# Low parts of layer A's weights by DMAs that add, in a two-layer decoder trunk on one core

## The chip, the cores and the metric

The kernel runs on one core of one Trainium2 chip. The metric is the device time of one execution in microseconds; the median of three runs before the change is 933.11 us (932.33 to 933.43).

## What is computed

x has 512 rows of 1024. Layer A is a retention layer with 4 heads, layer B a latent attention with 16 heads; each ends in a layer norm of a scaled residual sum. The change lies in layer A:

```python
def _retention_layer(x, w_in, w_out):
    b, s, _ = x.shape
    hproj = x @ w_in
    qk = H_A * DK_A
    q = hproj[..., :qk].reshape(b, s, H_A, DK_A)
    k = hproj[..., qk:2 * qk].reshape(b, s, H_A, DK_A)
    v = hproj[..., 2 * qk:2 * qk + WIDTH_A].reshape(b, s, H_A, DV_A)
    gate = hproj[..., 2 * qk + WIDTH_A:]
    q = _rope(q, ROPE_BASE_A)
    k = _rope(k, ROPE_BASE_A) * (DK_A ** -0.5)
    o = _chunkwise_retention(q, k, v)
    ...
    return (o * jax.nn.silu(gate)) @ w_out
```

All of it is float32; H_A = 4, DK_A = 256, DV_A = 512.

## The kernel before, in words

**Three products for one.** Every float32 matrix is split in two parts of a shorter float type: the high part is a cast, the low part what the cast left out. A product is then three matmuls of TensorE that add up in PSUM: high by high, high by low, low by high (`mm3`, lines 97 to 99; the first projection has its own loop, line 387).

**Weights.** All weights pass through the class `Weights` as tiles of 128 x 1024. For each, SP loads a staging tile `wst` (line 65, or 48 in `load`), ScalarE casts it to `whi` (line 66) and VectorE or GpSimd writes `wlo` = `wst` - `whi` (line 68). GpSimd gets every third tile, from the ninth on, unless its name is in `on_vector`. The pairs `whi`, `wlo` rotate through four buffers, so a tile's pair can be written once TensorE has done with the tile four earlier; staging has eight buffers in layer A. `get` hands a tile to its user and issues two tiles ahead.

**Layer A, head by head.** For the values and gates of a head (`values_and_gates`), x and the two weight blocks are cut in quarters, and seven products take the place of eight: p1, p6, p2, p5, p7, p4, p3 in this order, each of two weight tiles (24 matmuls). Some of them use sums of weights, built in staging tiles by `w_vg` (line 118): for p6, v0 = g0 - v0 and then t2 = g1 - v0; for p4, v1 = v1 - t2 (`last_sum`); for p7, g0 = g1 - g0. In head 0, t2 lies in the spare buffers `wsum`, which later hold s4, the fourth form of x. In head 0 these sums are VectorE's; in heads 1 to 3 GpSimd does the last two kinds. Forms of x (s1 to s4) are summed and split on VectorE and ScalarE. After p2 come the scores of the head (24 matmuls of 512 to 128 columns; `sf`, `sTh`, `sTl`), then p5, p7, p4, p3, the inner products (30 matmuls), and with `proj_qk` the query and key of the next head (`qk1` and on, four tiles of 24 matmuls), the transposes and the output projection (`o0` and on, four tiles). In head 0 the rows of x are loaded again for the residual (line 569), after the second of the next weight loads, and scaled by ScalarE (line 571).

**What sets the order.** The program is written head by head, and a scheduler that works from its own costs then fixes each engine's order of instructions, SP's and GpSimd's queues included. An engine goes through its list in order: what stands behind a waiting instruction waits too.

Of the kernel before, what the change touches and what calls it, by code (L numbers as in the profile page):

```python
# [8 lines left out]
F32 = mybir.dt.float32  # L9
BF16 = mybir.dt.bfloat16  # L10
F32R = mybir.dt.float32r
AF = mybir.ActivationFunctionType
ALU = mybir.AluOpType
# [6 lines left out]
H_A, DK_A, DV_A = 4, 256, 512  # L20
# [16 lines left out]
class Weights:  # L37
# [3 lines left out]
    def __init__(self, nc, stage, parts, ahead):  # L41
        self.nc, self.stage, self.parts, self.ahead = nc, stage, parts, ahead
        self.todo, self.ready, self.n, self.place = [], [], 0, {}
        self.on_vector = {f"p{i}.0" for i in range(1, 8)} | {f"p{i}.3" for i in (7, 4, 3)} | {"o3", "lat"}

    def load(self, ap):
        st = self.stage.tile([P, WC], F32, tag="wst", name="wst")
# [3 lines left out]
    def issue(self, between=None):  # L51


        nc = self.nc
        name, aps, n = self.todo.pop(0)
        st = aps() if callable(aps) else self.stage.tile([P, WC], F32, tag="wst", name="wst")
        pool, th, tl = self.place[name].pop(0) if self.place.get(name) else (self.parts, "whi", "wlo")
        hi = pool.tile([P, WC], F32R, tag=th, name="whi")
        lo = pool.tile([P, WC], F32R, tag=tl, name="wlo")
        for j, ap in enumerate(aps if isinstance(aps, list) else [aps]):  # L60
            sl = slice(j * n, (j + 1) * n)
            if j and between:
                between()
            if not callable(ap):
                self.last = nc.sync.dma_start(st[:, sl], ap)
            nc.scalar.copy(hi[:, sl], st[:, sl])  # L66
            eng = nc.gpsimd if self.n % 3 == 2 and self.n > EAGER and name not in self.on_vector else nc.vector
            eng.tensor_tensor(out=lo[:, sl], in0=st[:, sl], in1=hi.bitcast(F32)[:, sl], op=ALU.subtract)  # L68
        self.n += 1
        self.ready.append((name, hi, lo))  # L70
# [10 lines left out]
def trunk_kernel(ctx, tc, a):  # L81
    nc = tc.nc
    out = a["out"]
# [26 lines left out]
    def w_vg(h):  # L110

        v, g, s = a["w_v"], a["w_g"], {}

        def sub(out, x, y, eng):
            eng.tensor_tensor(out=out, in0=x, in1=y, op=ALU.subtract)  # L118
            return out

        def p1(t):
            s["v0", t] = W.load(v[4 * h + t])
            return s["v0", t]

        def p6(t):
            s["g0", t] = W.load(g[4 * h + t])
            s["g1", t] = W.load(g[4 * h + 2 + t])
            sub(s["v0", t], s["g0", t], s["v0", t], nc.vector)


            s["t2", t] = spare.pop(0) if spare else s["g1", t]
            return sub(s["t2", t], s["g1", t], s["v0", t], nc.vector)

        def p2(t):
            s["v1", t] = W.load(v[4 * h + 2 + t])
            return s["v1", t]

        def last_sum(t):
            return sub(s["v1", t], s["v1", t], s["t2", t], nc.gpsimd if h else nc.vector)

        def p5(t):
            if h:
                last_sum(t)
            return s["v0", t]

        def p7(t):
            if s["t2", t] is s["g1", t]:
                s["g1", t] = W.load(g[4 * h + 2 + t])
            return sub(s["g0", t], s["g1", t], s["g0", t], nc.gpsimd if h else nc.vector)

        def p4(t):
            return s["v1", t] if h else last_sum(t)

        def p3(t):
            return s["g1", t]

        def entry(f, t):
            return (f"{f.__name__}.{h}", lambda: f(t), 1024)

        return [entry(f, t) for f in (p1, p6, p2, p5, p7, p4, p3) for t in range(2)]  # L160

    spare = []

    order = [("qk0", [a["w_qk0"][2 * c], a["w_qk0"][2 * c + 1]], 512) for c in range(KX // 2)]
    for h in range(H_A):
        order += w_vg(h)
        if h + 1 < H_A:
            order += [(f"qk{h + 1}", a["w_qk"][4 * h + t], 1024) for t in range(4)]
        order += w_a("w_ao", "o", h)
# [23 lines left out]
    for p in range(NP):  # L193
        i, b = 2 * p, 2 * p + 1
# [123 lines left out]
    if True:  # L318
# [51 lines left out]
        qk, vv, sT, gs, oT, dec, ors = {}, {}, {}, {}, {}, {}, {}  # L370
# [210 lines left out]
        g1 = keep.tile([P, D], F32, tag="lng", name="g1")  # L581
# [107 lines left out]
    with tc.tile_pool(name="pb1", bufs=1) as p1:  # L689
# [33 lines left out]
        for c in range(4):  # L723
            wh, wl = W.get("ql0")
            for n in ORD:
                for j in range(2):
                    k = 2 * c + j
                    sl = slice(j * 512, (j + 1) * 512)
# [3 lines left out]
        for n in range(NT):  # L732
            y = p1.tile([P, QL], F32, tag="qn", name="qn", bufs=4)
# [5 lines left out]
        for c, ks in enumerate(((0, 1, 2), (3, 4, 5), (6, 7))):  # L739
            wh, wl = W.get("ql1")  # L740
            for n in range(NT):
                for j, k in enumerate(ks):
                    sl = slice(j * 320, (j + 1) * 320)
# [162 lines left out]
    for p in range(NP):  # L906
        i, b = 2 * p, 2 * p + 1
# [62 lines left out]
    st = p2.tile([P, 4, 6], F32, tag="ln_st4", name="ln_st4")  # L970
# [11 lines left out]
    for sl in (slice(0, 512), slice(512, 1024)):  # L982
        y = r[:, last, sl]
        nc.vector.scalar_tensor_tensor(out=y, in0=y, scalar=mv[:, 0:1], in1=g2[:, sl], op0=ALU.subtract, op1=ALU.mult)
    for sl, queue in ((slice(0, 512), nc.sync), (quarters[2], nc.scalar), (quarters[3], nc.sync)):
        y = r[:, last, sl]
# [101 lines left out]
```

## Time and profile before

| | |
|---|---|
| median of three runs | 933.11 us |
| the profiled execution | 931.95 us, its span 930.1 us |
| TensorE busy | 913.4 us (98%), 4553 matmuls |
| VectorE busy | 647.0 us (70%) |
| ScalarE busy | 356.9 us (38%) |
| GpSimd busy | 176.5 us (19%) |
| DMA | 97.45 MB, mean 105 GB/s |

PE is TensorE, PEld its weight loads, DVE VectorE, ACT ScalarE, POOL GpSimd, SP the engine that issues the loads. Times in rows are microseconds from the start of the span. Matmuls overlap (one starts before the last has ended), so a row's duration of 0.39 us is not the step from one to the next. Head 0's products end at 84 us, its projections at some 130; head 3's products begin near 318, and layer A ends near 400.

### The profile page before, as it was taken

Reading aid. Unit: us, or ns where it says so; the run is one execution under the profiler, and the core shown is the slowest. Engines: PE = TensorE matmul, PEld = TensorE weight load, DVE = VectorE, ACT = ScalarE, POOL = GpSimd, SP = SyncE. Lnnn points to the kernel's source line nnn. Section 1 sums busy time; section 2 is a strip of 40 time slices with the busy share of each in tenths; the row PEclk is TensorE's granted clock in tenths of the full one; section 3 lists DMA queues with packets and bytes.
Section 4 is the critical chain, followed back from the end, with each engine's and each line's share of the span. In section 5 each row is a group of like instructions: output and inputs, shape, how many; then the busy total and the mean of one; then the engine's idle time right before and its main releaser. Section 6 shows DMA issues by size and latency. Waiting matters only on the chain.

```text
span 930.1 us, 11970 instructions
## 1 busy us (share of the span) xinstructions
PE 913.4 (98%) x4553; PEld 774.6 (83%) x4553; DVE 647.0 (70%) x1117; ACT 356.9 (38%) x600; POOL 176.5 (19%) x108
## 2 busy tenths in 40 slices
PE   9989999999999999999999999999999999999996
PEld 6767888888888887888988888888888888888885
DVE  7998767866796689952477476564865648657577
ACT  6463334333433344222525443333433334334431
POOL 0001136212631250121312011010011011111204
PEclk9999999999999999999999999999999999999998
DMA  9164204420442050134143324242242422423212
GB/s 335 61 220 145 89 30 141 159 91 16 152 161 91 12 203 24 68 88 136 52 125 117 105 74 123 75 125 69 74 136 68 119 69 74 135 70 108 92 69 91
DMA packets 32362, 97.45 MB, mean 105 GB/s; under 512 B 4272, under 2 KB 4912, under 8 KB 32304
## 3 DMA queue, kind: packets, MB, share of 16 engines
q1 hardware_dynamic: 28800, 87.11, 27.8%
q10 hardware_dynamic: 3504, 9.57, 4.0%
q8 instruction: 36, 0.59, 0.3%
q14 instruction: 22, 0.18, 0.1%
HBM read 86.18 MB, written 2.10 MB: 95 GB/s over the span
## 4 chain that ended last, share of the span: by engine, by line
PE 81%; DVE 8%; issue 4%; POOL 3%; DMA 3%; ACT 1%; SPq 0%; DVEq 0%; POOLq 0%; ACTq 0%
PE ps L98 25%; PE ps L99 25%; PE ps L97 25%; DVE wlo L68 2%; PE ps L848 2%; POOL wst L118 1%; DMA wst<-in_w_v 1%; PE ps L825 1%; PE ps L826 1%; DMA r<-in_xT 1%; DMA r<-in_x 1%; PE ps L540 1%; POOL wlo L68 1%; PE ps L302 1%; DVE vl L103 0%
## 5 line engine op out<-in xcount | busy, mean ns | idle before, releaser
L66 ACT CAST whi<-wst 128x1024 fp32r<-128x1024 f32 (+3 forms) x181 | 173.2, 964 | 264.0 <-PE ps L98 89.1
L68 DVE TENSOR_TENSOR wlo<-wst,whi 128x1024 fp32r<-128x1024 f32 (+2 forms) x132 | 163.2, 1241 | 96.9 <-ACT whi L66 96.4
L68 POOL TENSOR_TENSOR wlo<-wst,whi 128x1024 fp32r<-128x1024 f32 (+3 forms) x49 | 110.6, 2257 | 615.8 <-ACT whi L66 584.6
L833 ACT ACTIVATE p<-ps,sm 128x512 f32<-128x512 f32 (+1 forms) x64 | 33.3, 525 | 66.6 <-DVE sm L830 66.5
L97 PE MATMUL ps<-qlt_h,whi 128*128 128x512 f32 x144 | 56.9, 395 | 0.0
L98 PE MATMUL ps<-qlt_l,whi 128*128 128x512 f32 x144 | 56.5, 392 | 0.0
L99 PE MATMUL ps<-qlt_h,wlo 128*128 128x512 f32 x144 | 56.4, 391 | 0.0
L97 PE MATMUL ps<-x1h,whi 128*128 128x512 f32 x128 | 50.6, 396 | 0.0
L97 PE MATMUL ps<-whi,oTh 128*128 128x512 f32 x128 | 50.2, 392 | 0.0
L99 PE MATMUL ps<-whi,oTl 128*128 128x512 f32 x128 | 50.0, 390 | 0.1
L98 PE MATMUL ps<-x1l,whi 128*128 128x512 f32 x128 | 50.0, 390 | 0.0
L99 PE MATMUL ps<-x1h,wlo 128*128 128x512 f32 x128 | 49.9, 390 | 0.0
L98 PE MATMUL ps<-wlo,oTh 128*128 128x512 f32 x128 | 49.8, 389 | 0.0
L97 PE MATMUL ps<-whi,ogh 128*128 128x512 f32 (+1 forms) x114 | 44.7, 392 | 0.0
L99 PE MATMUL ps<-whi,ogl 128*128 128x512 f32 (+1 forms) x114 | 44.1, 387 | 0.0
L98 PE MATMUL ps<-wlo,ogh 128*128 128x512 f32 (+1 forms) x114 | 44.0, 386 | 0.0
L98 PE MATMUL ps<-wlo,xTh 128*128 128x512 f32 x96 | 38.3, 399 | 1.6 <-DVE wlo L68 1.5
L899 DVE TENSOR_TENSOR r<-r,ps 128x512 f32<-128x512 f32 (+1 forms) x49 | 32.3, 670 | 10.4 <-PE ps L99 10.4
L97 PE MATMUL ps<-whi,xTh 128*128 128x512 f32 x96 | 37.8, 395 | 1.8 <-ACT whi L66 1.8
L99 PE MATMUL ps<-whi,xTl 128*128 128x512 f32 x96 | 38.1, 397 | 0.0
L97 PE MATMUL ps<-xTh,whi 128*128 128x512 f32 x96 | 37.6, 392 | 0.0
L99 PE MATMUL ps<-xTh,wlo 128*128 128x512 f32 x96 | 37.4, 389 | 0.0
(248 smaller groups left out, 2392.3 us busy)
## 6 DMA issues: line engine op xcount, KB each, us to landing
wst<-in_w_g SPq DMA_DIRECT2D x22, 512.0 KB, 3.2
wst<-in_w_v SPq DMA_DIRECT2D x16, 512.0 KB, 3.5
wst<-in_w_ao SPq DMA_DIRECT2D x16, 512.0 KB, 3.6
wst<-in_w_gb SPq DMA_DIRECT2D x16, 512.0 KB, 3.8
qr<-uv ACTq DMA_DIRECT2D x64, 128.0 KB, 2.4
wst<-in_w_bo SPq DMA_DIRECT2D x16, 512.0 KB, 3.6
wst<-in_w_qk SPq DMA_DIRECT2D x12, 512.0 KB, 3.7
wst<-in_w_q SPq DMA_DIRECT2D x16, 384.0 KB, 3.1
```

The source lines that it names most:

```text
L66: nc.scalar.copy(hi[:, sl], st[:, sl])
L68: eng.tensor_tensor(out=lo[:, sl], in0=st[:, sl], in1=hi.bitcast(F32)[:, sl], op=ALU.subtract)
L97: nc.tensor.matmul(ps, lhsT=lh, rhs=rh, start=start, stop=False)
L98: nc.tensor.matmul(ps, lhsT=lh, rhs=rl, start=False, stop=False)
L99: nc.tensor.matmul(ps, lhsT=ll, rhs=rh, start=False, stop=stop)
L118: eng.tensor_tensor(out=out, in0=x, in1=y, op=ALU.subtract)
L302: nc.tensor.transpose(out=ps[:, k * P : (k + 1) * P], in_=src[:, k * P : (k + 1) * P], identity=ident)
L540: nc.tensor.transpose(out=ps[:, k * P : (k + 1) * P], in_=gs[h][:, n, k * P : (k + 1) * P], identity=ident)
L825: nc.tensor.matmul(ps, lhsT=rh[:, qs], rhs=krp[:, :n], start=False, stop=False)
L833: nc.scalar.activation(pp, ps, AF.Exp, bias=sm[:, qb, 1:2], scale=SCALE_B, accum_out=sm[:, qb, 2:3])
L848: nc.tensor.transpose(out=ps[:, do : do + P], in_=pr[i][:, so : so + P], identity=ident)
L899: nc.vector.tensor_tensor(out=dst, in0=dst, in1=ps, op=ALU.add)
```

## The change

`by_dma` names 34 tiles: in head 0 those of p2, p5, p7, p4 and p3 (ten), the query and key tiles of heads 1 to 3 (twelve) and the output tiles of heads 0 to 2 (twelve). For them ScalarE writes -`whi` into `wlo` after the cast, and a DMA issued by GpSimd adds the weights onto it: from the staging tile, where that holds a sum or is used for one (head 0), else from the weights in memory. In head 0 the sums v1 - t2 and g1 - g0, four in all, are made alike: ScalarE negates the second operand where it lies, and a DMA adds one onto the other. All other p tiles of all heads go to VectorE, so that GpSimd computes no low part in layer A up to `lat`.

```diff
@@ Weights.__init__
-        self.on_vector = {f"p{i}.0" for i in range(1, 8)} | {f"p{i}.3" for i in (7, 4, 3)} | {"o3", "lat"}
+
+        self.on_vector = {f"p{i}.{h}" for i in range(1, 8) for h in range(H_A)} | {"o3", "lat"}
+        self.by_dma = {f"p{i}.0" for i in (2, 5, 7, 4, 3)} | {f"{nm}{h}" for h in range(H_A) for nm in ("qk", "o")} - {"qk0", "o3"}
@@ Weights.issue
             nc.scalar.copy(hi[:, sl], st[:, sl])
+            if name in self.by_dma:
+
+                nc.scalar.activation(lo[:, sl], hi.bitcast(F32)[:, sl], AF.Copy, scale=-1.0)
+                nc.gpsimd.dma_start(lo[:, sl], st[:, sl] if callable(ap) else ap, accum_op=ALU.add)
+                continue
             eng = nc.gpsimd if self.n % 3 == 2 and self.n > EAGER and name not in self.on_vector else nc.vector
             eng.tensor_tensor(out=lo[:, sl], in0=st[:, sl], in1=hi.bitcast(F32)[:, sl], op=ALU.subtract)
@@ w_vg
+        def sub_by_dma(out, x, y):
+
+            nc.scalar.activation(y, y, AF.Copy, scale=-1.0)
+            nc.gpsimd.dma_start(out, x if out is y else y, accum_op=ALU.add)
+            return out
+
         def last_sum(t):
-            return sub(s["v1", t], s["v1", t], s["t2", t], nc.gpsimd if h else nc.vector)
+            if h == 0:
+                return sub_by_dma(s["v1", t], s["v1", t], s["t2", t])
+            return sub(s["v1", t], s["v1", t], s["t2", t], nc.gpsimd)
@@ p7 in w_vg
-            return sub(s["g0", t], s["g1", t], s["g0", t], nc.gpsimd if h else nc.vector)
+            if h == 0:
+                return sub_by_dma(s["g0", t], s["g1", t], s["g0", t])
+            return sub(s["g0", t], s["g1", t], s["g0", t], nc.gpsimd)
```

The order moves on all engines. Three places, in head 0:

ScalarE ahead of p2. `whi_298` and `whi_320` are p6's tiles, `m_287` holds p1's results, `whi_340` and the tile after it are p2's. Before:

```order
L66 CAST whi_298<-wsum_168 128x1024
L471 COPY m_287<-ps_290 128x512
L66 CAST whi_320<-wsum_169 128x1024
L471 COPY m_287<-ps_291 128x512
L66 CAST whi_340<-wst_338 128x1024
L66 CAST whi_346<-wst_344 128x1024
```

Changed:

```order
L68 CAST whi_298<-wsum_168 128x1024
L147 ACTIVATE wst_314<-wst_314 128x1024
L147 ACTIVATE wsum_168<-wsum_168 128x1024
L488 COPY m_287<-ps_290 128x512
L68 CAST whi_320<-wsum_169 128x1024
L488 COPY m_287<-ps_291 128x512
L68 CAST whi_340<-wst_338 128x1024
L68 CAST whi_347<-wst_345 128x1024
L71 ACTIVATE wlo_341<-whi_340 128x1024
L71 ACTIVATE wlo_348<-whi_347 128x1024
```

Two negations of sums stand ahead of p1's copy, and p2's low parts are begun only after both casts.

GpSimd's queue, from its first work after the constants. `wlo_341` and `wlo_348` are p2's low parts, `wlo_416` and `wlo_433` p5's, `wlo_456` p7's first; `wst_338` and `wst_345` hold v1, `wsum` t2. DMASW2 counts the third adding DMA, `wlo_341`, and DMASW3 the fourth. Before, GpSimd did nothing in head 0 up to the third tile of `qk1`; its list went on with:

```order
L68 TENSOR_TENSOR wlo_757<-wst_755,whi_756 128x1024 [waits DMAHW7_49,Activation_49]
L262 TENSOR_TENSOR o_rs_686<-rs_t_704,mhalf_80 128x1 [waits DVE_49,Pool_49]
L262 TENSOR_TENSOR o_rs_686<-rs_t_722,mhalf_80 128x1 [waits DVE_49]
L262 TENSOR_TENSOR o_rs_686<-rs_t_737,mhalf_80 128x1 [waits DVE_49]
L262 TENSOR_TENSOR o_rs_686<-rs_t_749,mhalf_80 128x1 [waits DVE_49]
```

Changed:

```order
L148 DMA wst_292<-wst_294 128x1024 [waits DMAHW6_49,Activation_49]
L148 DMA wst_314<-wst_316 128x1024 [waits DMAHW1_49,DMAHW3_49,DMAHW0_49,Activation_49]
L72 DMA wlo_341<-wst_338 128x1024 [waits DVE_49,DMAHW1_49,PE_49,Activation_49]
L72 DMA wlo_348<-wst_345 128x1024 [waits DVE_49,DMAHW2_49,PE_49,Activation_49]
L148 DMA wst_338<-wsum_168 128x1024 [waits DMAHW3_49,DMASW2_49]
L72 DMA wlo_416<-wst_222 128x1024 [waits DVE_49,PE_49,Activation_49]
L72 DMA wlo_433<-wst_252 128x1024 [waits DVE_49,PE_49,Activation_49]
L148 DMA wst_345<-wsum_169 128x1024 [waits DMAHW5_49,DMAHW7_49,DMASW3_49,Activation_49]
L72 DMA wlo_456<-wst_292 128x1024 [waits DMASW0_49,PE_49,Activation_49]
```

The sum onto `wst_338` waits until p2's first low part has landed, and p5's low parts stand behind it.

VectorE and ScalarE between p2 and p4. VectorE before, from the scores' first bank on:

```order
L434 TENSOR_TENSOR sf_468<-ps_461,c_288 128x512
L68 TENSOR_TENSOR wlo_451<-wst_292,whi_450 128x1024
L68 TENSOR_TENSOR wlo_456<-wst_314,whi_455 128x1024
L103 TENSOR_TENSOR sTl_460<-sf_468,sTh_459 128x512
L103 TENSOR_TENSOR vl_506<-v_445,vh_505 128x512
L434 TENSOR_TENSOR sf_479<-ps_472,c_288 128x384
```

VectorE changed; DMASW7 counts the sum onto `wst_345`, which reads `wsum_169`, the buffer of `s4l`:

```order
L451 TENSOR_TENSOR sf_476<-ps_469,c_288 128x512 [waits DMAHW4_49,PE_49]
L110 TENSOR_TENSOR s4l_588<-gs_282,s4h_587 128x1024 [waits DMASW7_49,Activation_49]
L110 TENSOR_TENSOR sTl_468<-sf_476,sTh_467 128x512 [waits Activation_49]
L110 TENSOR_TENSOR vl_514<-v_449,vh_513 128x512 [waits Activation_49]
L451 TENSOR_TENSOR sf_487<-ps_480,c_288 128x384 [waits DVE_49]
```

ScalarE changed, from the scores' second bank to p4's first low part (`whi_551`, `wlo_552`):

```order
L109 CAST sTh_467<-sf_487 128x384
L109 CAST sTh_467<-sf_498 128x256
L588 ACTIVATE r_70<-r_70 128x1024
L68 CAST whi_551<-wst_338 128x1024
L109 CAST sTh_467<-sf_509 128x128
L71 ACTIVATE wlo_552<-whi_551 128x1024
```

The scaling of the first rows of x now stands ahead of p4's cast, and the fourth form of x ahead of most of the scores' work.

## Rows read from the trace of the kernel before

**Rows 1.** The page: span, and busy time of each engine.

```profile
span 930.1 us, 11970 instructions
PE 913.4 (98%) x4553; PEld 774.6 (83%) x4553; DVE 647.0 (70%) x1117; ACT 356.9 (38%) x600; POOL 176.5 (19%) x108
```

**Rows 2.** Windows: busy us of each engine (instructions), granted clock, DMA share, GB/s.

```profile
30.00:40.00 10.00, 10.00 (x46) 8.29 (x45) 10.00 (x13) 6.36 (x8) 0.00 (x0) 1.00 0.00 1
...
60.00:70.00 10.00, 6.63 (x21) 4.96 (x21) 9.96 (x11) 7.60 (x8) 0.00 (x0) 0.83 0.56 202
...
65.00:70.00 5.00, 5.00 (x17) 3.97 (x17) 4.96 (x7) 3.54 (x4) 0.00 (x0) 0.72 0.95 363
...
340.00:370.00 30.00, 28.08 (x126) 22.30 (x124) 29.79 (x47) 15.94 (x23) 1.10 (x2) 1.00 0.26 92
...
350.00:400.00 50.00, 48.06 (x231) 39.25 (x230) 49.56 (x86) 15.63 (x24) 6.15 (x8) 1.00 0.17 53
```

**Rows 3.** Timeline of PE in head 0: start, us, instruction, [idle before, releaser].

```profile
38.48 0.39 PE L97 MATMUL ps<-whi,xTh 128*128 128x512 f32 x1
...
43.69 0.39 PE L99 MATMUL ps<-whi,xTl 128*128 128x512 f32 x1
45.05 0.50 PE L97 MATMUL ps<-qkh 128*128 128x512 f32 x1 [0.97 <-ACT qkh L102]
...
59.73 0.39 PE L99 MATMUL ps<-whi,s3l 128*128 128x512 f32 x1
61.94 0.73 PE L97 MATMUL ps<-whi,xTh 128*128 128x512 f32 x2 [1.82 <-ACT whi L66]
64.22 0.69 PE L98 MATMUL ps<-wlo,xTh 128*128 128x512 f32 x1 [1.54 <-DVE wlo L68]
...
67.96 0.39 PE L99 MATMUL ps<-whi,xTl 128*128 128x512 f32 x1
...
77.73 0.39 PE L97 MATMUL ps<-vh,sTh 128*128 128x512 f32 x1
78.72 0.50 PE L98 MATMUL ps<-vl,sTh 128*128 128x512 f32 x1 [0.60 <-DVE vl L103]
...
84.10 0.39 PE L97 MATMUL ps<-xTh,whi 128*128 128x512 f32 x1
```

**Rows 4.** Timeline of DVE in head 0: p6's first low part, p2's two.

```profile
30.42 1.21 DVE L68 TENSOR_TENSOR wlo<-wsum,whi 128x1024 fp32r<-128x1024 f32 x1
...
35.62 2.35 DVE L68 TENSOR_TENSOR wlo<-wst,whi 128x1024 fp32r<-128x1024 f32 x2
```

**Rows 5.** Timeline of PE in head 3: first score, first output transposes.

```profile
333.67 0.39 PE L97 MATMUL ps<-qkh 128*128 128x512 f32 x1
...
367.42 0.66 PE L540 MATMUL ps<-ident,gs 128*128 128x128 f32 x4 [1.55 <-DVE gs L529]
```

**Rows 6.** Timeline of ACT in head 0: three casts, a scaling of x.

```profile
34.29 2.95 ACT L66 CAST whi<-wst 128x1024 fp32r<-128x1024 f32 x3
...
53.23 1.06 ACT L571 ACTIVATE r<-r 128x1024 f32<-128x1024 f32 x1
```

**Rows 7.** DMA issues by line: count, KB each, median us to landing.

```profile
wst<-in_w_g SPq DMA_DIRECT2D x22, 512.0 KB, 3.2
...
wst<-in_w_bo SPq DMA_DIRECT2D x16, 512.0 KB, 3.6
...
wst<-in_w_k SPq DMA_DIRECT2D x16, 256.0 KB, 2.7
...
r<-in_x SPq DMA_DIRECT2D x4, 512.0 KB, 4.8
```

**Rows 8.** Timelines of DVE and POOL in head 3, ahead of the scores.

```profile
334.33 6.92 DVE L68 TENSOR_TENSOR wlo<-wst,whi 128x1024 fp32r<-128x1024 f32 x3 [4.54 <-ACT whi L66]
341.17 1.48 DVE L434 TENSOR_TENSOR sf<-ps,c 128x512 f32<-128x512 f32 x3
...
321.50 2.40 POOL L68 TENSOR_TENSOR wlo<-wst,whi 128x1024 fp32r<-128x1024 f32 x1 [11.21 <-ACT whi L66]
```

## Prediction

> **What bounds the kernel now.** I read the page's totals first, then the time windows, TensorE's waits, TensorE's timeline at each wait, and the engine that ended it. TensorE is busy for 913.4 of 930.1 us [rows 1]: at most some 17 us of idle time are to be had, part of it at the two ends. The windows show where the middle loses: 60 to 70 us holds 21 matmuls where a full window holds 46, 350 to 400 us is 1.9 us short, and from 65 to 70 us the granted clock is 0.72 [rows 2]. (Matmuls overlap, so I count starts: 46 in 10 us is 0.2265 us each.)
>
> The timeline gives head 0's losses as start against the start due at that cadence [rows 3]: the scores at 45.05 instead of 43.92, one step after 43.69 (1.1); product p4: the matmul at 67.96 is the twelfth after 59.73 and was due at 62.45 (5.5: two waits of 1.8 and 1.5, and starts 0.42 apart over the nine intervals from 64.22, at the lower of the two clock levels, 1.2 GHz); 78.72 instead of 77.96 (0.8). Together 7.4 us: the next head's key projection starts at 84.10 and could start at 76.7. What ended these waits was ScalarE or VectorE: VectorE is busy for all of 30 to 40 us, and still catching up at 60 [rows 2, 4]. Head 3 repeats it smaller: its first output transposes wait 1.55 us for VectorE [rows 5].
>
> **What is taken off.** In head 0 VectorE loses ten low parts and four weight sums. Two low parts run from 35.62 for 2.35 us [rows 4], 1.17 us each, so 14 x 1.17 = 16 us of VectorE work go between 35 and 83 us. ScalarE gains 14 negations of 1024 columns. The ones it runs now over x cost 1.06 us [rows 6]; it is busy for 6.4 of the 10 us from 30 to 40 [rows 2], so I price them by their place. The 24 further adds (query and key of heads 1 to 3, output of heads 0 to 2) have cover: their weight tiles work for 24 matmuls (5.4 us) each and four buffers rotate, so a tile may take three tiles, 16 us, against two ScalarE steps and an add. They cost nothing unless an add takes over 14 us.
>
> **How long an adding DMA takes** from issue to landing (X below) no row shows. Plain loads of 256 KB land in 2.7 us and of 512 KB in 3.6 [rows 7]: 1.8 us grow with the bytes and 1.8 do not. An add can't be quicker than the copy: 3.6 below. If reading the target too doubles the part that grows, X is 5.4; two transfers in a row give 7.2, the upper end. I take 4.5, midway between the first two, because a plain load beside others took 4.8 [rows 7] and reading and writing may partly overlap.
>
> The Trainium skill, "Collectives: The Full Stack", section "The bandwidth ceiling: the fold count and why AG ≠ RS ≠ AR", speaks against the change: a DMA that adds reads two sources through one read path and so runs at half the rate. By that rule X is the 5.4 above and the sum below comes out 0.7 us slower instead of 2.4 us faster; no row here shows an adding DMA, so it stands among the rivals.
>
> **The new wait at p2.** In the changed order ScalarE negates the second sum of p6 before it copies the first results of p1, and casts both p2 tiles before it negates either. From the times of before: the negation must wait for VectorE's read of the sum, which began at 30.42 and took 1.21 us [rows 4], so it runs from 31.7 to 32.75; copy to 33.25; cast 33.2 to 34.2; copy to 34.7; the two p2 casts to 36.6 (0.96 apart, as 2.95 us for three now [rows 6]); the first negation ends at 37.6. The add issues at 37.65 and lands at 42.15. TensorE reaches p2 at 38.48 [rows 3], does two high products and wants the low part at 38.93. It waits **3.2 us** (X less 1.3), where before it waited for nothing.
>
> A wait that long lowers the clock: the 1.8 us wait at 60 us did, and full pace was back only by 67.96; the one of 1.55 us in head 3 did not [rows 3, 5]. In those 6 us, 0.42 apart, some 14 matmuls would start, each 0.19 us late: **2.6 us** (1.7 by the nine intervals alone; none if the wait stays short).
>
> **Behind it.** Call the landing Z. p2's first tile is done at Z+4.35 (ten matmuls at the lower clock), the second at Z+7.6 (22 matmuls, 5.0, and the 2.6). Only then are buffers free: ScalarE casts p7's first tile to Z+5.4, negates the second sum to Z+6.35, and its add lands at Z+10.9. GpSimd's queue is in order too: the sums over p2's tiles stand ahead of p5's low parts, and wait for p2's adds to land; p5's adds, issued by Z+2 behind the sum's, land by about Z+9 and are wanted at Z+11.8. VectorE's low part of the fourth form of x is written into the buffer of that second sum, so it waits to Z+10.9 and ends at 12.1; the score products behind it end at 14.1. ScalarE casts them, then scales the first rows of x. These were loaded after the next weights, which wait for p5's adds (SP's queue): issued from Z+9.3, 4.8 to land [rows 7], there by about Z+14, so the scaling ends at 15.55. Then p4's cast (16.5), a short cast, the negation (17.75), the add: Z+22.3. TensorE wants it at Z+22.9 (7.6; scores 4.2, what 76.7 leaves after 38.48 and 150 full matmuls; p5 and p7 10.9; one matmul). It fits with 0.6 us to spare. The same walk gives p4's second tile 0.4 us to spare, p3's first none, and p3's second, behind two tanh, **0.55 us** late.
>
> Sum for head 0: 76.7 + 3.2 + 2.6 + 0.55 = 83.05 against 84.10: 1.05 us gained. The old waits all go: at the scores VectorE is 2.3 us earlier, and p4 no longer waits for it. What is late next is the add itself.
>
> **Head 3.** VectorE stands full from 340 to 370 [rows 2] and starts on the scores at 341.17, though their first products began at 333.67 [rows 5, 8]. Just before, three low parts took 6.9 us, double their price, beside GpSimd's sums and low parts [rows 8]. GpSimd's low part at 321.50 and the one after it go; VectorE gets one or two tiles more ahead of the scores. The gain lies between nothing and the 2.3 us lost there; I take 1.4, over half, since GpSimd's sums end earlier and VectorE had 4.5 us idle ahead of those three [rows 8]. Heads 1 and 2 have no wait to lose; layer B keeps its order.
>
> **Sum:** 1.05 + 1.4 = 2.4 us. The profiled execution took 931.95 us (span 930.1) and the median of the three runs is 933.11; I take the difference from the median: **930.7 us**. A measurement of this kernel can tell about 0.2%, 1.9 us.
>
> **The rivals.** *The add is slow, and its delay is paid twice.* One mechanism: X enters once at p2, and again through GpSimd's queue (the sum's add), VectorE's wait, the x rows and p4's add. At X = 5.4 the wait at p2 is 4.1 and p4 and p3 come 2.8 us late: 76.7 + 4.1 + 2.6 + 2.8 = 86.2, 2.1 slower in head 0, net 0.7 slower, which is no change. At 7.2: 5.9 at p2, 6.6 behind it, the lower clock a second time: 94.4, net 8.9 slower, 942. From X = 5.7 on it decides for slower. For it: no spare time at p3, and three queues in order. (The rule of two reads of the Trainium skill, cited above, is its 5.4.) Against: the DMA engines carry nothing from 30 to 40 us [rows 2], so p2's adds have them alone.
>
> *The wait stays short and the clock stays up.* With X at 3.2 the wait is 1.9 us, about where the clock fell or not; then head 0 ends at 78.6, 5.5 us sooner, and with head 3 the whole is 7 us faster: 926. For it: the gate weights' 512 KB land in 3.2 us [rows 7]. Against: an add does more than a load.
>
> *Nothing to see:* X between 4.75 and 5.7, the gains and the new wait cancel: 931.2 to 935. That the change doesn't do what it says can be left out: the order shows 38 adding DMAs on GpSimd's queue and no GpSimd low part in layer A.
>
> **How the numbers follow.** X below 4.75 with the lower clock (929 to 931, my forecast): 0.38. Clock kept: 0.09. Cancelled: 0.21. Slow add: 0.32. So faster 0.47, same 0.21, slower 0.32. The range takes the low end from the kept clock, 926, and reaches up to the slow add near its upper bound, 7 us: 941. Outside lie adds of 7 us or more and gains beyond both terms.
>
> **What would show it.** In the changed profile: the first adding DMAs' time from issue to landing (the whole sum hangs on it); one TensorE wait at p2's first low product near 39 us of 2 to 5 us, released by a DMA, and a granted clock below 1 right after; no wait at 45 and none of 5 us at p4; VectorE's share between 35 and 85 us down by some 16 us; the key projection of head 1 starting near 83 us; the transposes of head 3 waiting under 1 us. I am wrong in mechanism if p2 doesn't wait, or if p4 or p3 wait longer than p2; wrong in size if X is not near 4.5.

## The result and the profile after

The changed kernel took 941.8 us (median of four runs, 941.33 to 942.0) where the kernel before took 932.87 beside it (932.33 to 933.43): a ratio of 1.0095, 95% interval 1.0077 to 1.0112. It is slower by about 9 us, just above the predicted range. The profiled execution took 942.0 us, its span is 940.2.

The page's totals (they answer to [rows 1]) and its two largest DMA queues:

```profile
span 940.2 us, 12080 instructions
PE 915.7 (97%) x4553; PEld 775.8 (83%) x4553; DVE 619.7 (66%) x1099; ACT 394.7 (42%) x638; POOL 161.0 (17%) x126
...
q1 hardware_dynamic: 28800, 87.11, 27.4%
q0 software_dynamic: 5472, 19.93, 11.6%
```

The relief came as meant: VectorE works 27 us less. TensorE's idle time grew all the same. The windows of the changed kernel, which answer to [rows 2] (same columns), show where:

```profile
30.00:40.00 10.00, 8.94 (x39) 6.74 (x37) 9.90 (x14) 9.33 (x11) 2.58 (x3) 1.00 0.65 123
40.00:50.00 10.00, 7.50 (x26) 6.04 (x27) 6.12 (x8) 7.47 (x9) 3.54 (x5) 0.83 1.05 196
50.00:60.00 10.00, 8.85 (x47) 7.41 (x45) 4.06 (x8) 4.47 (x7) 1.66 (x2) 1.00 1.05 219
60.00:70.00 10.00, 6.33 (x24) 4.35 (x24) 3.12 (x8) 3.66 (x7) 0.00 (x0) 1.00 1.02 358
70.00:80.00 10.00, 4.47 (x11) 3.52 (x12) 3.88 (x6) 8.57 (x10) 3.44 (x4) 0.68 0.98 236
...
350.00:400.00 50.00, 49.80 (x231) 40.76 (x230) 49.34 (x83) 20.72 (x29) 4.18 (x6) 1.00 0.28 94
```

The DMA share, the last column but one, is full from 40 us on, while VectorE is half idle. From 350 to 400 us 1.7 of the 1.9 us that were missing are there: head 3's wait is gone.

TensorE's timeline in head 0 (to hold against [rows 3]; the first matmul of p2, each wait, and the next head's key product):

```profile
38.44 0.61 PE L104 MATMUL ps<-whi,xTh 128*128 128x512 f32 x2
42.49 0.50 PE L105 MATMUL ps<-wlo,xTh 128*128 128x512 f32 x1 [3.44 <-DMA wlo<-wst]
...
58.46 0.39 PE L104 MATMUL ps<-whi,s3h 128*128 128x512 f32 x1
61.74 0.50 PE L105 MATMUL ps<-wlo,s3h 128*128 128x512 f32 x1 [2.89 <-DMA wlo<-wst]
...
65.53 0.50 PE L105 MATMUL ps<-wlo,s3h 128*128 128x512 f32 x1 [0.76 <-DMA wlo<-wst]
...
68.86 0.50 PE L104 MATMUL ps<-whi,xTh 128*128 128x512 f32 x1 [0.52 <-ACT whi L68]
75.53 0.80 PE L105 MATMUL ps<-wlo,xTh 128*128 128x512 f32 x1 [6.17 <-DMA wlo<-wst]
...
96.34 0.39 PE L104 MATMUL ps<-xTh,whi 128*128 128x512 f32 x1
```

The key product starts at 96.34 instead of 84.10, 12.2 us later. The span grew by 10.1, so everything behind gained 2.1. Without any wait it could start at 76.2: 38.44, five products of 24 matmuls at 0.2267, the step of the 30 inner products here (5.44 each), the scores as they ran (3.75) and the inner products (6.8). The 20.1 us that are missing lie at p2 (5.3: done at 49.21, due at 43.88), p7 (5.0, counted to p4's first matmul, so with the 0.5 us that this one waits for p4's cast), p4 (8.9, by the same count to p3's first matmul at 83.18) and p3 (0.9). Each is a wait and, behind p2 and p4, some matmuls 0.43 us apart: the granted clock is 0.83 from 40 to 50 and 0.68 from 70 to 80 us, so part of each stretch ran at 1.2 GHz.

The adding DMAs as GpSimd issued them:

```profile
37.84 1.80 POOL L72 DMA_DIRECT2D wlo<-wst  x2 [5.61 <-DVE ropeB L426]
42.74 0.85 POOL L148 DMA_DIRECT2D wst<-wsum  x1 [3.09 <-DVE rope L431]
43.27 2.08 POOL L72 DMA_DIRECT2D wlo<-wst  x2
48.99 0.86 POOL L148 DMA_DIRECT2D wst<-wsum  x1 [3.63 <-ACT wsum L147]
49.94 0.86 POOL L72 DMA_DIRECT2D wlo<-wst  x1
52.78 0.86 POOL L72 DMA_DIRECT2D wlo<-wst  x1 [1.98 <-ACT wlo L71]
70.26 0.86 POOL L72 DMA_DIRECT2D wlo<-wst  x1 [16.62 <-ACT wlo L71]
```

Held against TensorE's waits: p2's first add, issued at 37.84, lets the matmul go at 42.49, 4.65 later. p7's first, issued at 49.94, takes until 61.74, **11.8 us**; its second until 65.53, 12.7. The same kind of transfer, the same bytes, on the same queue. The rows in between show why p4 is late too; first VectorE, then ScalarE:

```profile
56.73 1.23 DVE L110 TENSOR_TENSOR s4l<-gs,s4h 128x1024 fp32r<-128x1024 f32 x1 [5.27 <-DMA wst<-wsum]
```

```profile
59.66 0.82 ACT L109 CAST sTh<-sf 128x384 fp32r<-128x384 f32 x2 [5.35 <-DVE sf L451]
66.81 1.06 ACT L588 ACTIVATE r<-r 128x1024 f32<-128x1024 f32 x1 [6.34 <-DMA r<-in_x]
67.78 1.03 ACT L68 CAST whi<-wst 128x1024 fp32r<-128x1024 f32 x1
68.71 0.29 ACT L109 CAST sTh<-sf 128x128 fp32r<-128x128 f32 x1
68.91 1.05 ACT L71 ACTIVATE wlo<-whi 128x1024 fp32r<-128x1024 f32 x1
```

VectorE waits for the second sum's add, ScalarE for VectorE, and then 6.3 us for the x rows, which stand in its order ahead of p4's cast and negation. p4's add can only be issued at 70.26.

What the DMA engines carried from 42.7 to 65.5 us in the changed kernel (queue: packets, MB, share of 16 engines; then issues with KB each and median us to landing):

```profile
q0 software_dynamic: 960, 3.47, 83.1%
q1 hardware_dynamic: 486, 1.80, 20.5%
...
wlo<-wst POOLq DMA_DIRECT2D x4, 512.0 KB, 10.6
r<-in_x SPq DMA_DIRECT2D x4, 512.0 KB, 12.4
wst<-in_w_qk SPq DMA_DIRECT2D x3, 512.0 KB, 11.2
```

The two shares make the whole. The adds take four fifths of the engines for two thirds of the bytes, and loads that the change doesn't touch are late: the next key weights land after 11.2 us, where such loads took 3.7 before. The x rows land after 12.4 us instead of 4.8 [rows 7], but these two figures don't differ by the adds alone: before, two of the four loads were issued at 48.4 and two at 63.1 us; now all four go out from 53.8 us on, one behind the other, behind two loads of key weights.

### The profile page after: what moved, and what is told of

The parts are those of the page before. It is cut to its first block, busy times and chain, and to the rows that moved or that the text cites. A ratio compares the mean times of both kernels' runs of the same rounds, so it can differ in the third digit from the quotient of the medians.

```text
span 940.2 us, 12080 instructions
## 1 busy us (share of the span) xinstructions
PE 915.7 (97%) x4553; PEld 775.8 (83%) x4553; DVE 619.7 (66%) x1099; ACT 394.7 (42%) x638; POOL 161.0 (17%) x126
## 4 chain that ended last, share of the span: by engine, by line
PE 80%; issue 7%; DVE 5%; DMA 5%; POOL 2%; ACT 1%; SPq 0%; DVEq 0%; POOLq 0%; ACTq 0%
PE ps L105 25%; PE ps L106 25%; PE ps L104 25%; DMA wlo<-wst 2%; PE ps L865 2%; DVE wlo L75 1%; DMA r<-in_xT 1%; PE ps L842 1%; PE ps L843 1%; DMA wst<-in_w_g 1%; PE ps L557 1%; POOL wst L125 1%; PE ps L319 0%; POOL wlo L75 0%; ACT whi L68 0%
## 5 line engine op out<-in xcount | busy, mean ns | idle before, releaser
L75 DVE TENSOR_TENSOR wlo<-wst,whi 128x1024 fp32r<-128x1024 f32 (+3 forms) x118 | 147.5, 1253 | 82.5 <-ACT whi L68 81.8
L75 POOL TENSOR_TENSOR wlo<-wst,whi 128x1024 fp32r<-128x1024 f32 (+3 forms) x29 | 60.7, 2092 | 398.9 <-ACT whi L68 374.0
L125 POOL TENSOR_TENSOR wst<-wst 128x1024 f32<-128x1024 f32 x12 | 34.4, 2891 | 75.2 <-DVE wlo L75 75.2
L916 DVE TENSOR_TENSOR r<-r,ps 128x512 f32<-128x512 f32 (+1 forms) x49 | 32.4, 671 | 10.5 <-PE ps L106 10.4
```

The lines of the kernel that those rows point to most:

```text
L916: nc.vector.tensor_tensor(out=dst, in0=dst, in1=ps, op=ALU.add)
```

## The experiments

**The theory:** the loss is head 0's own and has two parts. One is p2's wait as predicted. The other is that from 43 us on the 16 DMA engines are full, because an added byte takes them about twice as long as a copied one; so adds, sums and x rows all come late. **Rivals:** the adds of heads 1 to 3 cost as well; the chain of three in-order queues costs this whatever the DMA does; all later waits are p2's delay handed on.

### Which part of the change: two halves

Head 0 back on VectorE, the rest as changed:

```diff
-        self.by_dma = {f"p{i}.0" for i in (2, 5, 7, 4, 3)} | {f"{nm}{h}" for h in range(H_A) for nm in ("qk", "o")} - {"qk0", "o3"}
+        self.by_dma = {f"{nm}{h}" for h in range(H_A) for nm in ("qk", "o")} - {"qk0", "o3"}
...
-            if h == 0:
-                return sub_by_dma(s["v1", t], s["v1", t], s["t2", t])
-            return sub(s["v1", t], s["v1", t], s["t2", t], nc.gpsimd)
+            return sub(s["v1", t], s["v1", t], s["t2", t], nc.gpsimd if h else nc.vector)
...
-            if h == 0:
-                return sub_by_dma(s["g0", t], s["g1", t], s["g0", t])
-            return sub(s["g0", t], s["g1", t], s["g0", t], nc.gpsimd)
+            return sub(s["g0", t], s["g1", t], s["g0", t], nc.gpsimd if h else nc.vector)
```

> Head 0's ten low parts and four sums go back to VectorE; the 24 adding DMAs of heads 1 to 3 stay, and GpSimd still makes no low part in layer A. Theory (all of the loss lies in head 0; the adds of heads 1 to 3 are hidden and head 3 gains 2 us): head 1's key product starts near 84.1 us as before the change, no TensorE wait in heads 1 to 3, 931 us, ratio to before 0.998. Rival (the adds of heads 1 to 3 cost something too): 933 us or more.

Measured: 928.7 us against 931.87 beside it, ratio 0.9956 (0.9938 to 0.9974). The key product:

```profile
82.87 0.39 PE L104 MATMUL ps<-xTh,whi 128*128 128x512 f32 x1
```

There is no wait in heads 1 to 3, though the key weights' adds take 11.1 us to land there. So the 24 adds of heads 1 to 3 with GpSimd's low parts gone are a gain: 1.2 us in head 0 (among them the wait of 0.6 at 78.72, which is gone, and 0.2 at p4), and 2.3 behind it (span 926.6 less 82.87, against 930.1 less 84.10). It is 2 us better than the theory said.

Head 0 alone, the others by the old rule:

```diff
-        self.on_vector = {f"p{i}.{h}" for i in range(1, 8) for h in range(H_A)} | {"o3", "lat"}
-        self.by_dma = {f"p{i}.0" for i in (2, 5, 7, 4, 3)} | {f"{nm}{h}" for h in range(H_A) for nm in ("qk", "o")} - {"qk0", "o3"}
+        self.on_vector = {f"p{i}.0" for i in range(1, 8)} | {f"p{i}.3" for i in (7, 4, 3)} | {"o3", "lat"}
+        self.by_dma = {f"p{i}.0" for i in (2, 5, 7, 4, 3)}
```

> The reverse: only head 0's ten low parts and four sums by adding DMA; query, key and output weights of heads 1 to 3 by VectorE and GpSimd by the old rule. Theory (the loss is head 0's own): head 1's key product starts near 96.3 us, head 3's wait of 1.5 us is back, 944 us, ratio to before 1.012. Rival (the loss needs the adds of the next head's key weights beside it): key product before 93 us, under 941.

Measured: 943.18 us, ratio 1.0118 (1.01 to 1.0137). The key product:

```profile
95.23 0.39 PE L104 MATMUL ps<-xTh,whi 128*128 128x512 f32 x1
```

Head 3's wait of 1.5 us is back, and the span less the key product is 846.2, as before the change (846.0). The loss is head 0's own, and 11 us of it; the rival is out.

### Is it the DMA engines' time: copies in place of adds

```diff
-                nc.gpsimd.dma_start(lo[:, sl], st[:, sl] if callable(ap) else ap, accum_op=ALU.add)
+                nc.gpsimd.dma_start(lo[:, sl], st[:, sl] if callable(ap) else ap)
...
-            nc.gpsimd.dma_start(out, x if out is y else y, accum_op=ALU.add)
+            nc.gpsimd.dma_start(out, x if out is y else y)
```

> Every adding DMA becomes a plain copy of the same bytes on the same queue, in the same order with the same waits; the addition is left out. Theory (what costs is the DMA engines' time: an added byte takes them about twice a loaded one, 183 against 388 GB/s by the shares of the changed kernel, and from 43 to 66 us they are asked for 28 us of work): the 512 KB step takes 1.4 instead of 2.8 us of all engines, the first wait (3.4 us) falls to about 2.2, those at p7 (3.65) to under 1, that at p4 (6.2) to 2 to 3; the key product starts near 89 us, 934 to 936 us. Rival (the chain of GpSimd's queue, ScalarE's negations and the buffers costs this whatever the DMA does): within 1.5 us of the changed kernel's 941.8.

Measured: 931.24 us, ratio to before 0.9988 (0.9977 to 0.9999): all of the loss is gone with nothing changed but the addition. The adding queue from 26 to 95 us, in the changed kernel and then with copies:

```profile
q0 software_dynamic: 2242, 8.20, 64.1%
```

```profile
q0 software_dynamic: 2594, 9.45, 37.3%
```

For 512 KB (0.524 MB) that is 0.524 / 8.20 x 0.641 x 69 us = **2.83 us** of all 16 engines for an add, and 1.43 for a copy. TensorE's waits with copies:

```profile
41.02 0.50 PE L105 MATMUL ps<-wlo,xTh 128*128 128x512 f32 x1 [1.76 <-DMA wlo<-wst]
...
57.43 0.50 PE L105 MATMUL ps<-wlo,s3h 128*128 128x512 f32 x1 [1.64 <-DMA wlo<-wst]
...
66.46 0.73 PE L105 MATMUL ps<-wlo,xTh 128*128 128x512 f32 x1 [3.25 <-DMA wlo<-wst]
```

Each is about half of what it was, and the clock stays full behind the first. The rival (queues and buffers alone) wanted 941.8. The theory was too careful: it said 89 us for the key product, which came at 85.65. The chain is still there, at half its length.

This run takes two things away at once: a copy needs half of the engines' time, and it also lands sooner by itself (2.98 us from issue to the waiting matmul, against 4.65). And it corrects the reading of the x rows above:

```profile
r<-in_x SPq DMA_DIRECT2D x4, 512.0 KB, 11.4
```

With no add anywhere they still take 11.4 us to land. What changed for them is when they are issued, at 47.7 us instead of 53.8: the key weights ahead of them in SP's queue wait for p5's transfers.

### The x rows: later, and not at all

Loads and scaling written behind the transposes (the block is moved as it stands):

```diff
             if h == 0:
-                with tc.issue_after(W.last.ins):
...
             inner(h, ORD)
             proj_qk(h + 1, 0)
             transposes(h, ORD)
+            if h == 0:
+                with tc.issue_after(W.last.ins):
...
```

> The loads of the x rows and ScalarE's scaling of them are written behind head 0's transposes instead of ahead of its inner products; all adds as in the changed kernel. Theory (the x rows cost twice: 5.4 us of the full DMA engines' time ahead of p7's adds, and their late landing holds ScalarE, so p4's cast and negation): p7's waits fall from 3.65 to about 1, p4's from 6.2 to under 1.5, p2's 3.4 stays; 932 to 935 us. Rival (an add's own latency, paid at p2 and again behind it, as in the prediction's rival; x rows not in it): p4 still waits over 4 us, 939 or more.

Measured: 943.15 us, ratio 1.0115 (1.0096 to 1.0134). Neither theory said this: p4's wait fell to 2.0, where the first said under 1.5, but the old wait came back at p3, and p7 still waits 2.84.

```profile
61.22 0.50 PE L105 MATMUL ps<-wlo,s3h 128*128 128x512 f32 x1 [2.84 <-DMA wlo<-wst]
...
73.49 0.50 PE L105 MATMUL ps<-wlo,xTh 128*128 128x512 f32 x1 [1.99 <-DMA wlo<-wst]
...
82.68 0.80 PE L105 MATMUL ps<-wlo,s4h 128*128 128x512 f32 x1 [6.17 <-DMA wlo<-wst]
```

The releaser on ScalarE is the one seen before, two casts later in its order: ahead of p3's first cast now.

```profile
73.95 1.06 ACT L591 ACTIVATE r<-r 128x1024 f32<-128x1024 f32 x1 [9.28 <-DMA r<-in_x]
```

So the wait goes with the scaling of the x rows, wherever that stands in ScalarE's order. And p7's add, which lets its matmul go at 61.22, is late although the x rows are issued only from 65.17 on in this run: their share of the engines is not what makes p7 wait. That part of the theory was wrong, and with it the total.

The loads left out:

```diff
-                with tc.issue_after(W.last.ins):
-                    for n in range(NT):
-                        nc.sync.dma_start(r[:, n, :], a["x"][:, n, :])
```

> The x rows are not loaded at all (four loads of 512 KB left out; ScalarE scales what stands in that buffer, so the output lacks x); all adds as in the changed kernel. Theory (from 43 to 82 us the DMA engines are the bound, and the late x rows hold ScalarE ahead of p4's or p3's negations): 5.4 us less of their time and nothing that holds ScalarE; p7's waits fall from 3.65 to about 1, those at p4 and p3 together from 7.3 to under 2; key product near 88 us, 932 to 934. Rival (buffers and the order of GpSimd's queue alone set p7's and p4's adds): 939 or more.

Measured: 936.46 us, ratio to before 1.0045 (1.0028 to 1.0061): 5 us better than the changed kernel (key product at 91.43), between the two forecasts. The wait of 6.2 is gone: p4 and p3 wait 1.43, 0.72, 0.47 and 1.01, 3.6 together where the theory said under 2. p7 still waits 2.93, where it said about 1:

```profile
63.49 0.50 PE L105 MATMUL ps<-wlo,s3h 128*128 128x512 f32 x1 [2.93 <-DMA wlo<-wst]
```

The second sum's add is still ahead of it and VectorE and ScalarE still wait for that (ScalarE idle 4.42 at 61.00). The x rows are thus worth about 5 us of the loss, at p4, where ScalarE no longer waits for them. Their four loads take about as much of the engines (4 x 1.39 = 5.6; at 10 to 20 us, loads alone, 3.92 MB took 104.1% of 10 us), but that this time is what costs is not shown: p7's wait hardly moved.

### Taking adds away one kind at a time

The four sums back on VectorE, the ten low parts still added by DMA:

```diff
-            if h == 0:
-                return sub_by_dma(s["v1", t], s["v1", t], s["t2", t])
-            return sub(s["v1", t], s["v1", t], s["t2", t], nc.gpsimd)
+            return sub(s["v1", t], s["v1", t], s["t2", t], nc.gpsimd if h else nc.vector)
...
-            if h == 0:
-                return sub_by_dma(s["g0", t], s["g1", t], s["g0", t])
-            return sub(s["g0", t], s["g1", t], s["g0", t], nc.gpsimd)
+            return sub(s["g0", t], s["g1", t], s["g0", t], nc.gpsimd if h else nc.vector)
```

> The four sums of head 0 go back to VectorE; its ten low parts stay with adding DMAs. Theory (DMA engines full): four adds fewer are 11 us less of their time, of which two fall before 36 us, where they are not full, so some 5.7 us less from 43 us on; p2's wait stays near 3.3, p7's falls under 1.5, p4's to 2 to 4; 934 to 937. Rival (VectorE is the bound of head 0 again as soon as it gets 4.7 us of work): VectorE shown as releaser of p4's wait, no better than 940.

Measured: 936.6 us, ratio 1.0049 (1.0034 to 1.0064): the total as the theory said. p7's wait is 1.30; p4's, at 5.67, is longer than expected: ScalarE still waits 5.9 us for x rows that land after 10.5. All waits are released by DMAs, none by VectorE.

p2 back on VectorE:

```diff
-        self.by_dma = {f"p{i}.0" for i in (2, 5, 7, 4, 3)} | {f"{nm}{h}" for h in range(H_A) for nm in ("qk", "o")} - {"qk0", "o3"}
+        self.by_dma = {f"p{i}.0" for i in (5, 7, 4, 3)} | {f"{nm}{h}" for h in range(H_A) for nm in ("qk", "o")} - {"qk0", "o3"}
```

> p2's two low parts go back to VectorE; the other eight low parts and the four sums of head 0 stay with adding DMAs. Theory (two costs: p2's wait with its lower clock, about 6 us, and behind it the DMA engines' 28 us of work from 43 to 66, which now has 5.7 less in it but is wanted 6 us sooner): no wait at 39 and full clock to the scores, p7 still waits 2 to 3 us and p4 5 to 6; key product near 90 us, 935 to 937. Rival (the prediction's: all later waits are p2's delay handed on): the waits at p7 and p4 go too, 930 or less.

Measured: 938.48 us, ratio 1.0063 (1.0046 to 1.008); key product at 92.74. No wait at 39, yet 3.6 us at the key product are all that this brings.

```profile
58.77 0.50 PE L105 MATMUL ps<-wlo,s3h 128*128 128x512 f32 x1 [1.36 <-DMA wlo<-wst]
...
64.60 0.79 PE L104 MATMUL ps<-whi,xTh 128*128 128x512 f32 x1 [3.04 <-ACT whi L68]
71.36 0.80 PE L105 MATMUL ps<-wlo,xTh 128*128 128x512 f32 x1 [5.96 <-DMA wlo<-wst]
```

p4 waits 9 us in all, behind a wait of ScalarE of 9.98 us for the x rows. So p4's wait is not p2's delay handed on, and the third rival falls there; at p7 the wait did fall, from 3.65 to 1.36, with the sums' adds landed early. The size was off by some 2 us.

### What early adds cost, and a kernel that beats both

Only the two last sums of head 0 by DMA (the weights are there early, in this run the adds go out at 36.91 and 38.28 us; the sums are wanted at p4):

```diff
-        self.by_dma = {f"p{i}.0" for i in (2, 5, 7, 4, 3)} | {f"{nm}{h}" for h in range(H_A) for nm in ("qk", "o")} - {"qk0", "o3"}
+        self.by_dma = {f"{nm}{h}" for h in range(H_A) for nm in ("qk", "o")} - {"qk0", "o3"}
...
         def p7(t):
...
-            if h == 0:
-                return sub_by_dma(s["g0", t], s["g1", t], s["g0", t])
-            return sub(s["g0", t], s["g1", t], s["g0", t], nc.gpsimd)
+            return sub(s["g0", t], s["g1", t], s["g0", t], nc.gpsimd if h else nc.vector)
```

> Of head 0 only the two last sums (second value weights minus the running sum) by adding DMA; its low parts and the other two sums by VectorE; the adds of heads 1 to 3 stay. Theory (an add that is issued tens of us before its result is wanted is free, and VectorE's sums at 59.5 us were what held p4): the waits at p4 fall from 3.1 us to under 1 and the lower clock behind them goes; key product near 78.5 us, 924 to 926. Rival (VectorE is late for other reasons, and p4's low part waits all the same): like the run with head 0 wholly on VectorE, 928.7.

Measured: 924.58 us, ratio 0.9921 (0.9906 to 0.9936), key product at 78.61; the waits at p4 are gone.

All four sums by DMA, every low part of head 0 by VectorE:

```diff
-        self.by_dma = {f"p{i}.0" for i in (2, 5, 7, 4, 3)} | {f"{nm}{h}" for h in range(H_A) for nm in ("qk", "o")} - {"qk0", "o3"}
+        self.by_dma = {f"{nm}{h}" for h in range(H_A) for nm in ("qk", "o")} - {"qk0", "o3"}
```

> All four sums of head 0 by adding DMA, its low parts by VectorE; the adds of heads 1 to 3 stay. Theory (early adds are free): VectorE has 4.7 us less, so the wait at the scores (0.9) goes too; key product near 77.5 us, 923 to 925. Rival (ScalarE's negations at 27 to 32 us delay its casts for p1 and p6, or p7's cast waits for the sums): a new wait before 40 or at 58 us, 926 or more.

Measured: **923.15 us, ratio to before 0.9907 (0.9893 to 0.9922)**. One wait of 0.25 is left in head 0:

```profile
44.57 0.50 PE L104 MATMUL ps<-qkh 128*128 128x512 f32 x1 [0.25 <-ACT qkh L109]
...
77.15 0.39 PE L104 MATMUL ps<-xTh,whi 128*128 128x512 f32 x1
```

The adds are issued at 27.83, 30.68, 36.65 and 38.02, in a stretch in which the DMA engines had next to nothing to do before (6% from 26 to 38 us), and ScalarE casts their results 14 to 17 us after their issue. From 60 to 70 us TensorE is full at full clock:

```profile
60.00:70.00 10.00, 10.00 (x46) 8.29 (x45) 8.42 (x12) 8.67 (x11) 1.33 (x2) 1.00 0.93 308
```

To this kernel p2's two low parts added by DMA:

```diff
-        self.by_dma = {f"{nm}{h}" for h in range(H_A) for nm in ("qk", "o")} - {"qk0", "o3"}
+        self.by_dma = {f"p{i}.0" for i in (2,)} | {f"{nm}{h}" for h in range(H_A) for nm in ("qk", "o")} - {"qk0", "o3"}
```

> The four sums and p2's two low parts by adding DMA, the other low parts of head 0 by VectorE; beside the run with the four sums alone (923.15 us) this prices one add that is wanted as soon as its weights are cast. Theory (the prediction's step at p2: X less 1.3, and the lower clock behind it): a wait of 3.2 to 3.5 us at 39, matmuls 0.42 apart for some 3 to 6 us behind it, key product near 82.5, 928 to 929. Rival (a single late add is made up later, since nothing else is near its limit): under 926.

Measured: 927.14 us, ratio 0.9943 (0.9929 to 0.9958).

```profile
42.94 0.79 PE L105 MATMUL ps<-wlo,xTh 128*128 128x512 f32 x1 [3.39 <-DMA wlo<-wst]
...
83.25 0.39 PE L104 MATMUL ps<-xTh,whi 128*128 128x512 f32 x1
```

Two adds wanted at once cost one wait of 3.4 and, with the lower clock behind it (0.60 from 45 to 50 us), 6.1 us at the key product (83.25 against 77.15). In this execution nothing makes it up later, but it is the slowest of the four (928.69); in the medians the difference is 4 us, below the 5 to 6 expected.

## Why the prediction was wrong

It forecast 930.7, 2.4 us faster; the kernel is 9 slower. Step by step:

- **What bounds the kernel before**: right. Head 0's 7.4 us and head 3's wait were VectorE's: the kernel that takes head 0's four sums and the query, key and output low parts of heads 1 to 3 off VectorE, but no low part of head 0, brings the key product to 77.15 and the whole to 923.15. One reading was off, with no effect: 46 matmuls in 10 us would be 0.217 us each, since a window also counts those that reach over its ends. The step used, 0.2265, is the one that the starts show.
- **The wait at p2** (X − 1.3 = 3.2, lower clock 2.6): right. 3.44 measured, with X at 4.65 where 4.5 was taken. The lower clock took 1.7 us (22 matmuls from 42.49 to 49.21), and 3.0 in the run with sums and p2 alone. p2 came 5.3 us late in all where 5.8 was forecast.
- **Behind it**: this is the step that failed. "p4 lands at Z+22.3 and is wanted at Z+22.9" took 4.5 us for every add and 4.8 for the x rows, as though each went alone. With Z at 42.49 the second sum's add came at Z+14.2 instead of Z+10.9. The x rows were issued at Z+11.3 instead of Z+9.3 and took 12.4 us, so ScalarE went on at Z+24.3 instead of Z+14, and p4's first add landed at Z+33.0. p7's adds were not priced at all; TensorE waited 3.65 us for them. Of the 20.1 us that head 0 lost, p2's 5.3 and most of p3's 0.9 were foreseen; p7's 5.0 and p4's 8.9 were not. The prediction's own sign says the same: it would be wrong in mechanism if p4 waited longer than p2, and p4's wait was 6.17 against 3.44.
- **What stood in its place.** At p7 it is work, not latency: from 42.7 to 65.5 us six adds and seven loads were asked for, 6 x 2.83 + 7 x 1.39 = 26.7 us of all engines in 22.8, and the engines were still busy with p2's second add. An estimate from the same 2.83: that add is done at 45.3, the next five, of which p7's first is the last, at 59.5; with some of the loads served between them the measured 61.74 is near. At p4 it is ScalarE's wait for the x rows: without them 1.43 and 0.72 us are left of the 6.17, and with their scaling moved the 6.17 come back at p3. The 4.8 us were read from a kernel that issues these loads two by two (4.8 to 6.1 us wherever head 0's low parts are VectorE's). Four together took 9.2 to 12.4 us, and 11.4 with copies.
- **The rule of the Trainium skill** ("Collectives: The Full Stack", section "The bandwidth ceiling: the fold count and why AG ≠ RS ≠ AR"): it says of the transfers of a ring collective that an add needs two source reads and so runs at half the rate of a copy. The runs agree for a kernel's own adds: 2.83 against 1.43 us, 1.98 to 1; from 110 to 330 us, with the weights from DRAM, it is 2.9 against 1.65 (copies: 8.93 MB in 12.8% of 220 us), 1.8 to 1. The prediction had it and used it for one add's latency only, 0.9 us more; its weight lies in the rate, which the rule is about.
- **The rival of the slow add** had the right order and came out at the measured total (+8.9, 942), but by luck: it put 5.9 us of waiting at p2, where 3.44 were measured, and 6.6 behind it, where 14.8 were lost. An add alone takes 4.65, not 7.2, and the delay isn't p2's paid twice, for without p2's add p4 still waits 9 us.
- **Heads 1 to 3 cost nothing unless an add takes over 14 us**: right, they take 5.6 to 11 us there and no wait is left. **Head 3's gain** of 1.4: 2.1 measured for everything behind head 0 (2.3 in the run with head 0 on VectorE), of which 1.7 lie between 350 and 400 us.

What stays open is how much of the x rows' lateness is the full engines and how much that four loads go out together behind two others, and what the order of the queues would cost by itself. Copies remove the whole loss, but they relieve the engines and shorten each transfer at once. The chain of waits is what turns late transfers into idle time of TensorE, and no run took the chain away with the engines left full.

## What to carry to other kernels

Price a DMA twice: by its latency where somebody waits for it, and by its share of the DMA engines' time, summed over all transfers asked for in the stretch; where that sum passes the stretch's length, transfers there come late, also those that the change doesn't touch (here the loads of key weights, 11.2 us instead of 3.7). And take a load's landing time from a place where it is issued as the new order will issue it: four loads in one go are not four single ones. An adding DMA counts double in that sum. It is a good place for work that is ready early and wanted late (sums of weights: 923.15 us with the four sums added by DMA against 928.7 without), and a poor one for the last step ahead of the engine that bounds the kernel.

## What was not expected of the hardware

- An adding DMA of 512 KB takes 2.83 us of all 16 engines, a copy on the same queue 1.43. Whether the other operand comes from SBUF or from DRAM makes little difference: from 110 to 330 us, where all adds read DRAM, the queue took 2.9 us for each (9.96 MB in 25.1% of 220 us):

```profile
q0 software_dynamic: 2737, 9.96, 25.1%
```

- Its issue holds GpSimd for 0.86 us, a plain copy's for 0.53 (the run with copies).
- A copy within SBUF on this queue let the matmul go 2.98 us after its issue (38.04 to 41.02), below the 3.6 of a load that the prediction took as the floor for X.
